# A hybrid decoder trunk on one core: the branch for overfull experts moves from behind the experts to in front of them

## Chip, cores and metric

The kernel runs on one core of a Trainium2 chip. The metric is the device time of one execution in microseconds, as the median over several runs.

## What is computed

Two decoder layers over 512 tokens of width 1024 in float32. Layer 0 mixes tokens by a gated delta rule, layer 1 by sparse attention. Behind each mixer stand a scaled residual, a layer norm, and a mixture of experts: of 16 experts in 4 groups every token takes the two best of its best group, each with hidden width 256.

```python
def hier_moe(x, w_grp, b_grp, w_rt, b_rt, w_gate, w_up, w_down):
    ...
    gate = jnp.sum(jax.nn.one_hot(expert_id, MOE_EXPERTS, dtype=jnp.float32) * top_w[..., None], axis=1)
    def step(acc, e_in):
        wg, wu, wd, ge = e_in
        hdn = jax.nn.silu(xt @ wg) * (xt @ wu)
        return acc + ge[:, None] * (hdn @ wd).astype(jnp.float32), None
```

The reference computes every expert for every token with a gate that is mostly zero; the kernel computes an expert only for the tokens that chose it.

## The kernel before, in words

A matrix product in float32 is made of three passes: each operand is split into a high part (a cast on ScalarE, `split`, L243) and the rest (a subtraction on VectorE or POOL, L252), and TensorE multiplies high by high, low by high and high by low (`mm3`, L276 to L278). In the trace wh and wl are the parts of gate and up weights, dh and dl of down weights, hgh and hgl of the gathered tokens.

`choose` (L907) picks two experts per token on VectorE and gives every token a slot in its expert; an expert has HOT = 128 slots, and tokens past the 128th have a slot number of 128 or more (`spos`). `moe` (L1113) then makes the lists of tokens (`idx`, L1119) and the largest number of tokens of any expert (`cm`, and `cmi` as an integer, L1124 to L1128). After that come the 16 experts in a software pipeline. `expert` (L1034) is a generator; each `go` advances it by a step: gather of its 128 tokens from d_h by an indirect DMA on POOL (L1039), transposes (L1049) with hgh and hgl behind them (L1053, L1054), gate and up (L1058), the activation (L1064 to L1066), its transposes (L1071), down (L1087), the product with the gate weight (L1095), and a scatter that adds the rows to the accumulator `d_acc` in HBM (L1101). The last experts (three in layer 0, two in layer 1, `late`) keep their rows in SBUF (L1089, L1090); `moe_finish` (L1332) brings them to the tokens by one-hot matmuls (L1350 in layer 0, L1387 in layer 1), adds them to h (L1355, L1394) and norms. h has by then been loaded from d_h and the accumulator has been added to it by a DMA from POOL (`addacc`, L1206 to L1213).

Weights come in loads of 1 MB on SP's queue (`load`, L1172; two issues for gate and up in L198, one for down in L208) into 13 raw buffers: three in the ring "raw", seven in "raw2", three in "raw3". Which one a load takes is worked out in `raw_slot` (L225); of the first five loads (gate and up of experts 0 and 1, down of expert 0) all take "raw2". From expert 3 on a load also waits until the load two before has landed (`paced`). The parts wh and wl have four buffers each, dh and dl two.

Inside each engine a scheduler orders the instructions at compile time by its own estimate, apart from those that `keep_in_program_order` holds in the order written. The parts of the first expert's weights (L1198, L1199) are held like this, and behind the fourth of them eight one-hots of 128x128 on VectorE (`slot_onehots`, L1143), which give the gate weight of each slot (`slot_weights`, L991).

Tokens past slot 128 are treated in a branch (L1280 to L1313) that stands behind all experts. Each engine loads `cmi` into a register and compares it with HOT. The body computes, for the slots 128 to 511 in three rounds of 128, the token lists, then loops over the experts, loads the weights again, and writes the rows to a buffer `d_yo` in HBM; after the loop every token gathers its own rows from there and adds them to h. The tiles of the body come out of the same rings as those around it. An engine that skips the body runs a few semaphore instructions instead (also put down to L1281), by which its semaphores get the counts that the body would have given them; those of SP wait for the DMA queues, those of POOL for its own DMAs. No instruction of another part stands between those of the body.

What ends a layer: in layer 0 `prefetch` (L1842) loads the first weights of the next stage from ScalarE's queue (L1844) ahead of the branch in the text, and `moe_finish` stands behind it; in layer 1 `moe_finish` writes the output.

## Time and profile before

| | us |
|---|---|
| median of 3 runs | 1187.27 |
| the runs | 1184.38, 1187.27, 1199.31 |
| profiled execution | 1185.92 |
| its span, first to last instruction | 1184.1 |
| experts of layer 0 (first gather to last late output) | 418.3 to 597.0 |
| experts of layer 1 | 972.4 to 1151.5 |

The profile is of one execution. PE is TensorE's matmuls, PEld its weight loads, DVE VectorE, ACT ScalarE, POOL GpSimd, SP SyncE; a name with q (PEq, PEldq, DVEq) is that engine's queue, which runs loads of registers, compares and semaphores, and these are not counted as busy. A row of the timeline gives start, duration, engine, line, operation, output and inputs, the number of instructions that are merged into it, and in brackets how long the engine had stood idle and what ended that. A row of the waits gives who waited for what, the total in us, how often, and the longest. A row of a line (its own view) gives the number of instructions, the shortest, median and longest duration in ns, and the first and last start in us.

### The profile page before, as it was taken

The numbers are of one execution on the slowest core, as the hardware profiler recorded it, in microseconds if no ns is written. First come the engines' busy times: TensorE is split into PE (matmuls) and PEld (weight loads), VectorE is DVE, ScalarE is ACT, GpSimd is POOL, SyncE is SP. The second block draws the span as 40 slices with busy tenths as digits, with TensorE's granted clock in tenths as the row PEclk, the third lists the DMA queues.
The fourth block names the chain that finished last, engine by engine and source line by source line (L and its number), as shares of the span: only waits on it lengthen the run. The fifth ranks groups of instructions, "written<-read, shape, count | busy, mean of one in ns | idle before, by whom it ended". The sixth has DMA issues, their size and how long they took to land. (4 is left out here: it accounts for less than half of the span.)

```text
span 1184.1 us, 16377 instructions
## 1 busy us (share of the span) xinstructions
PE 1068.6 (90%) x5565; PEld 843.7 (71%) x5565; DVE 837.4 (71%) x1511; ACT 609.9 (52%) x1085; POOL 540.2 (46%) x456
## 2 busy tenths in 40 slices
PE   6898999999999769999978999999999949989974
PEld 4677888788787557777766867667776837777763
DVE  3797777556563779999984224687785477999975
ACT  3532433232441259888722243477884036888862
POOL 0623873301002239888623213045545035888854
PEclk9998999999999979999999999999999978999997
DMA  6532434431126898999872582211115867899963
GB/s 211 174 102 78 112 96 119 163 97 39 36 72 191 290 324 280 297 311 304 249 214 84 149 249 99 71 37 28 37 49 157 306 211 266 286 288 307 332 147 97
DMA packets 110079, 206.01 MB, mean 174 GB/s; under 512 B 34473, under 2 KB 65321, under 8 KB 105892
## 3 DMA queue, kind: packets, MB, share of 16 engines
q1 hardware_dynamic: 96180, 178.18, 45.4%
q0 software_dynamic: 9584, 19.36, 7.2%
q10 hardware_dynamic: 4224, 7.34, 2.2%
q8 instruction: 47, 0.77, 0.3%
q14 instruction: 44, 0.36, 0.1%
HBM read 190.66 MB, written 35.21 MB: 191 GB/s over the span
## 5 line engine op out<-in xcount | busy, mean ns | idle before, releaser
L243 ACT CAST wh<-raw 128x1024 fp32r<-128x1024 f32 (+3 forms) x218 | 205.5, 949 | 189.3 <-PE mm L277 106.2
L252 DVE TENSOR_TENSOR wl<-raw,wh 128x1024 fp32r<-128x1024 f32 (+2 forms) x173 | 228.2, 1335 | 74.5 <-ACT wh L243 55.0
L276 PE MATMUL mm<-xh,wh 128*128 128x512 f32 (+2 forms) x400 | 165.9, 415 | 4.2 <-ACT wh L243 4.2
L278 PE MATMUL mm<-xh,wl 128*128 128x512 f32 (+2 forms) x400 | 162.9, 408 | 0.9 <-DVE wl L252 0.9
L277 PE MATMUL mm<-xl,wh 128*128 128x512 f32 (+2 forms) x400 | 163.4, 409 | 0.0
L252 POOL TENSOR_TENSOR wl<-raw,wh 128x1024 fp32r<-128x1024 f32 (+1 forms) x37 | 101.3, 2739 | 50.3 <-ACT wh L243 38.8
L1721 POOL TENSOR_SCALAR s<-s,st,gate 128x256 f32<-128x256 f32 (+2 forms) x96 | 64.5, 684 | 90.2 <-PE mm L1698 45.3
L276 PEld LDWEIGHTS mm<-xh,wh 128*128 128x128 f32 (+2 forms) x400 | 75.9, 190 | 24.8 <-ACT wh L243 4.8
L278 PEld LDWEIGHTS mm<-xh,wl 128*128 128x128 f32 (+2 forms) x400 | 75.7, 189 | 18.9 <-DVE wl L252 1.4
L277 PEld LDWEIGHTS mm<-xl,wh 128*128 128x128 f32 (+2 forms) x400 | 75.8, 189 | 16.3
L252 POOL TENSOR_TENSOR dl<-raw,dh 128x1024 fp32r<-128x1024 f32 x29 | 71.1, 2452 | 31.3 <-ACT dh L243 30.6
L1709 DVE CUSTOM_DVE_ANT_0 s<-mm,bias 128x128 f32<-128x128 f32 (+3 forms) x128 | 60.2, 481 | 24.3 <-PE tp L1726 20.8
L252 DVE TENSOR_TENSOR dl<-raw,dh 128x1024 fp32r<-128x1024 f32 x35 | 75.7, 2171 | 1.8 <-ACT dh L243 1.8
L1713 ACT ACTIVATE s<-s,st 128x128 f32<-128x128 f32 (+3 forms) x128 | 71.4, 559 | 8.8 <-DVE st L1709 8.4
L1101 POOL DMA_INDIRECT d_acc<-ye,idx x27 | 55.6, 2061 | 41.2 <-ACT ehh L1074 16.4
L243 ACT CAST dh<-raw 128x1024 fp32r<-128x1024 f32 x64 | 66.7, 1046 | 4.9 <-PE mm L278 1.3
L1039 POOL DMA_INDIRECT hg<-d_h,idx x32 | 56.8, 1776 | 17.1 <-ACT wh L243 7.5
L777 POOL TENSOR_TENSOR ln_m<-ln_m,mh 128x1 f32<-128x1 f32 x16 | 15.9, 991 | 102.9 <-DVE ln_m L776 102.9
L278 PE MATMUL mm<-wh,hgl 128*128 128x512 f32 x128 | 52.9, 413 | 11.0 <-DVE hgl L1054 11.0
L1726 PE MATMUL tp<-cst,s 128*128 128x128 f32 x320 | 55.2, 274 | 0.5 <-ACT cpt L1678 0.2
L1697 PE MATMUL mm<-kh,q 128*128 128x256 f32 (+2 forms) x128 | 53.9, 422 | 0.3 <-DVE st L1709 0.2
L276 PE MATMUL mm<-wh,hgh 128*128 128x512 f32 x128 | 52.6, 411 | 0.0
(505 smaller groups left out, 2682.1 us busy)
## 6 DMA issues: line engine op xcount, KB each, us to landing
raw<-in_moe_w_down_dram SPq DMA_DIRECT2D x32, 1024.0 KB, 6.9
raw<-in_moe_w_gate_dram SPq DMA_DIRECT2D x64, 512.0 KB, 6.5
raw<-in_moe_w_up_dram SPq DMA_DIRECT2D x64, 512.0 KB, 7.0
raw<-in_gdn_w_in_dram SPq DMA_DIRECT2D x16, 1024.0 KB, 6.9
d_h<-raw SPq DMA_DIRECT2D x10, 512.0 KB
d_sk<-d_rr ACTq DMA_DIRECT2D x4, 1280.0 KB, 25.8
bc<-d_gc SPq DMA_DIRECT2D x16, 256.0 KB
d_acc<-u SPq DMA_DIRECT2D x8, 512.0 KB, 5.6
```

The costliest lines, as they stand in the source:

```text
L243: p(nc.scalar.copy(h, src))
L252: p(e.tensor_tensor(l, src, h, op=OP.subtract))
L276: nc.tensor.matmul(ps, a[0], b[0], start=start, stop=False)
L277: nc.tensor.matmul(ps, a[0], b[1], start=False, stop=False)
L278: nc.tensor.matmul(ps, a[1], b[0], start=False, stop=stop)
L1039: nc.gpsimd.indirect_dma_start(out=hg, out_offset=None, in_=d_h, bounds_check=T - 1, oob_is_err=False, in_offset=bass.IndirectOffsetOnAxis ...
L1101: i = nc.gpsimd.indirect_dma_start(out=dst, out_offset=bass.IndirectOffsetOnAxis(ap=to, axis=0), in_=ye, in_offset=None, compute_op=OP.add ...
L1697: nc.tensor.matmul(a.ps[:, :W], q[:, c], kh[:, :W], start=True, stop=False)
L1709: nc.vector.tensor_tensor_reduce(out=a.p, in0=a.ps[:, :a.W], in1=bias[a.head][:, (3 - a.i) * P:], scale=-1.0, scalar=3e38, op0=OP.add, op1 ...
L1713: nc.scalar.activation(a.p, a.p, AF.Exp, bias=a.st[:, 0, a.i:a.i + 1], scale=-1.0, accum_out=a.st[:, 1, a.i:a.i + 1])
L1721: en.tensor_scalar(a.p, a.p, a.st[:, 2, a.i:a.i + 1], N["gate"][:, a.i, k:k + 1], op0=OP.mult, op1=OP.mult)
L1726: nc.tensor.transpose(a.ps[:, j * P:(j + 1) * P], a.p[:, j * P:(j + 1) * P], self.ident)
```

## The change

The branch moves from behind the experts to between the gather of the first expert and that of the second; five loads of weights are issued ahead of it (`load` skips those that have been made). Its body is now the function `overflow`. In place of the buffer `d_yo` and the gathers out of it, the body computes the gate weight of every slot past 128 (24 more one-hots and small matmuls in three rounds, kept in `d_gs`), and its experts scale their rows and add them to the accumulator by the same scatter as the others. Its weights take the three buffers of the ring "raw", and its gathers the second of the two token buffers. The scatter in the body isn't held in program order (`pin=None`).

```diff
--- before.py
+++ after.py
@@ -1024,6 +1024,38 @@
         half = lambda i: lambda w=None: self.raw((g[:, 4 * i:4 * i + 4, :], u[:, 4 * i:4 * i + 4, :]), (KC, EH), w)
         return half(0), half(1), lambda w=None: self.raw(src[2].rearrange("(p j) c -> p j c", j=2), (2, D), w)
 
+    def overflow(self, ep, R, d_h, hg):
+
+        nc, tc, layer = self.nc, self.tc, R["layer"]
+        NJ = CAP // HOT
+        d_io = self.t(self.dr, [P, NJ, E], f"d_io{layer}", I32)
+        d_gs = self.t(self.dr, [P, NJ, E], f"d_gs{layer}")
+        for j in range(1, NJ):
+            pi, pw = self.bank("tp", 3), self.bank("tp", 3)
+            for tt in range(NT):
+                self.slot_ids(ep, R, tt, j, pi[:, :E])
+            for tt in range(NT):
+                for i in range(2):
+                    o, pj = self.t(ep, [P, P], "oh32", bufs=2 * NT), self.t(ep, [P, 1], "opj", bufs=2)
+                    nc.vector.tensor_scalar(pj, R["spos"][:, i, tt:tt + 1], float(-j * HOT), None, op0=OP.add)
+                    nc.vector.tensor_scalar(o, self.c["iota"], pj, None, op0=OP.is_equal)
+                    nc.tensor.matmul(pw[:, :E], o, R["A"][:, i, tt, :], start=tt + i == 0, stop=tt + i == NT)
+            io, gw = self.t(ep, [P, E], "oi", I32, 2), self.t(ep, [P, E], "og", bufs=2)
+            nc.vector.tensor_scalar(io, pi[:, :E], float(NOWHERE), None, op0=OP.add)
+            nc.vector.tensor_copy(gw, pw[:, :E])
+            nc.sync.dma_start(d_io[:, j, :], io)
+            nc.sync.dma_start(d_gs[:, j, :], gw)
+        with tc.For_i(0, E, 1) as e:
+            r = [a(self.slot(1)) for a in self.expert_weights(layer, e)]
+            gu = [self.split_gu(r[i // 2], i, ["dve"] * 4) for i in range(4)]
+            dn = self.split_dn(r[2], ["dve"] * 2)
+            for j in range(1, NJ):
+                io, gw = self.t(ep, [P, 1], "oi1", I32, 2), self.t(ep, [P, 1], "og1", bufs=2)
+                nc.sync.dma_start(io, d_io[:, j, bass.ds(e, 1)])
+                nc.sync.dma_start(gw, d_gs[:, j, bass.ds(e, 1)])
+                for _ in self.expert(ep, hg, gu, lambda: dn, io, d_h, R["acc"], io, gs=gw, pin=None):
+                    pass
+
     def split_gu(self, raw, i, lo=LO):
         r = raw.rearrange("p (a b) c -> p a b c", a=2)
         return self.spl2(r[:, :, i % 2 * 2:i % 2 * 2 + 2, :], lo[i])
@@ -1100,7 +1132,7 @@
                 yield
                 i = nc.gpsimd.indirect_dma_start(out=dst, out_offset=bass.IndirectOffsetOnAxis(ap=to, axis=0), in_=ye,
                                              in_offset=None, compute_op=OP.add, bounds_check=T - 1, oob_is_err=False)
-                if CFG["spin"]:
+                if CFG["spin"] and pin is not None:
                     self.tc.keep_in_program_order(i)
 
     def onehot(self, R, tt, e, pin=False):
@@ -1126,8 +1158,6 @@
         nc.vector.tensor_reduce(cm, ps[:, :E], axis=AX.X, op=OP.max)
         cmi = self.t(mp, [P, 1], "cmi", I32)
         nc.vector.tensor_copy(cmi, cm)
-        d_yo = self.t(self.dr, [E * (CAP - HOT), D], f"d_yo{layer}")
-        d_io = self.t(self.dr, [P, CAP // HOT, E], f"d_io{layer}", I32)
         with self.pool("ep", "right") as ep:
             X, R["late"] = {}, []
             self.t(ep, [P, D], "ye", bufs=CFG["ye"])
@@ -1171,9 +1201,10 @@
 
             def load(e, n):
                 if e < E:
-                    if n == 0:
+                    if e not in raws:
                         raws[e] = list(self.expert_weights(layer, e))
-                    raws[e][n] = raws[e][n]()
+                    if callable(raws[e][n]):
+                        raws[e][n] = raws[e][n]()
 
             def spread():
                 for i in range(4):
@@ -1183,9 +1214,12 @@
                     nc.scalar.copy(gb[:, c], ps)
 
             raws = {}
-            load(0, 0)
-            load(0, 1)
+            for e, n in ((0, 0), (0, 1), (1, 0), (1, 1), (0, 2)):
+                load(e, n)
             tokens(0)
+            n = nc.values_load(cmi[0:1, 0:1], min_val=0, max_val=T)
+            with tc.If(n > HOT):
+                self.overflow(ep, R, d_h, hgs[1])
             for e in range(1, CFG["hg"]):
                 tokens(e)
             if CFG["o32e"] == 1:
@@ -1277,40 +1311,6 @@
             for i in range(2):
                 R["pre"](i)
             self.pace = 0
-            n = nc.values_load(cmi[0:1, 0:1], min_val=0, max_val=T)
-            with tc.If(n > HOT):
-                for j in range(1, CAP // HOT):
-                    pi = self.bank("tp", 3)
-                    for tt in range(NT):
-                        self.slot_ids(ep, R, tt, j, pi[:, :E])
-                    io = self.t(ep, [P, E], "oi", I32, 2)
-                    nc.vector.tensor_scalar(io, pi[:, :E], float(NOWHERE), None, op0=OP.add)
-                    nc.sync.dma_start(d_io[:, j, :], io)
-                with tc.For_i(0, E, 1) as e:
-                    a, b, d = self.expert_weights(layer, e)
-                    gu = []
-                    for r in (a, b):
-                        r = r(self.slot(2))
-                        gu += [self.split_gu(r, len(gu) + i, ["dve"] * 4) for i in range(2)]
-                    dn = self.split_dn(d(self.slot(2)), ["dve"] * 2)
-                    for j in range(1, CAP // HOT):
-                        io = self.t(ep, [P, 1], "oi1", I32, 2)
-                        nc.sync.dma_start(io, d_io[:, j, bass.ds(e, 1)])
-                        for _ in self.expert(ep, hgs[j % CFG["hg"]], gu, lambda: dn, io, d_h, d_yo[bass.ds(e * (CAP - HOT) + (j - 1) * HOT, HOT), :]):
-                            pass
-                f8 = lambda a: a.rearrange("p a b -> p (a b)")
-                go, so = self.t(ep, [P, 2, NT], "ogo"), self.t(ep, [P, 2, NT], "oso")
-                soi = self.t(ep, [P, 2, NT], "osoi", I32)
-                nc.vector.tensor_scalar(f8(so), f8(R["spos"]), -float(HOT), 0.0, op0=OP.add, op1=OP.max)
-                nc.vector.scalar_tensor_tensor(f8(soi), f8(R["sbase"]), (CAP - HOT) / HOT, f8(so), op0=OP.mult,
-                                               op1=OP.add)
-                nc.vector.scalar_tensor_tensor(f8(go), f8(R["spos"]), float(HOT), f8(R["gate"]), op0=OP.is_ge, op1=OP.mult)
-                for tt in range(NT):
-                    for i in range(2):
-                        y = hgs[i]
-                        nc.gpsimd.indirect_dma_start(out=y, out_offset=None, in_=d_yo,
-                                                     in_offset=bass.IndirectOffsetOnAxis(ap=soi[:, i, tt:tt + 1], axis=0))
-                        nc.vector.scalar_tensor_tensor(h[tt], y, go[:, i, tt:tt + 1], h[tt], op0=OP.mult, op1=OP.add)
             self.ring = 1
 
     @contextmanager
```

## Rows read from the trace of the kernel before

**Rows 1.** The page, part 1: busy time, share of the span, instructions of each engine.

```profile
PE 1068.6 (90%) x5565; PEld 843.7 (71%) x5565; DVE 837.4 (71%) x1511; ACT 609.9 (52%) x1085; POOL 540.2 (46%) x456
```

**Rows 2.** Waits of TensorE, 950 to 1158 us: total, times, longest.

```profile
PE mm L1387 <- PEq L1281: 6.2, 1, 6.2
...
PE tp L1049 <- DMA hg<-d_h,idx: 6.1, 1, 6.1
```

**Rows 3.** Waits of TensorE, 404 to 600 us.

```profile
PE tp L1049 <- DMA hg<-d_h,idx: 8.8, 1, 8.8
...
PE o L1350 <- DVEq L1281: 2.1, 1, 2.1
```

**Rows 4.** Line L1281, layer 1: duration ns min/median/max, first and last start.

```profile
L1281 PEldq COMPARE_BRANCH  x1: 6159/6159/6159, 1149.6 to 1149.6; - x1
...
L1281 DVEq COMPARE_BRANCH  x1: 68/68/68, 1151.8 to 1151.8; - x1
...
L1281 PEldq EVENT_SEMAPHORE  x1: 51/51/51, 1155.8 to 1155.8; - x1
```

**Rows 5.** Line L1281, layer 0.

```profile
L1281 SPq EVENT_SEMAPHORE  x8: 17/17/17, 570.9 to 600.5; - x8
...
L1281 PEldq COMPARE_BRANCH  x1: 367/367/367, 594.5 to 594.5; - x1
...
L1281 ACTq COMPARE_BRANCH  x1: 45/45/45, 596.6 to 596.6; - x1
```

**Rows 6.** Timeline, end of layer 1: start, duration, engine, line.

```profile
1149.83 1.63 DVE L1090 SCALAR_TENSOR_TENSOR raw<-mm,rgs,raw 128x512 fp32r<-128x512 f32 x2 [2.14 <-ACT raw L1089]
...
1156.17 5.97 PE L1387 MATMUL mm<-raw,raw 128*128 128x512 f32 x16 [6.21 <-PEq L1281]
...
1158.25 0.69 DVE L1394 TENSOR_TENSOR raw<-mm,raw 128x512 f32<-128x512 f32 x1 [6.78 <-PE mm L1387]
```

**Rows 7.** Line L1394, the closing norm's first add in layer 1.

```profile
L1394 DVEq EVENT_SEMAPHORE  x1: 49/49/49, 1155.5 to 1155.5; - x1
```

**Rows 8.** Timeline of VectorE, end of layer 0.

```profile
596.27 0.75 DVE L1090 SCALAR_TENSOR_TENSOR raw<-o,rgs,raw 128x512 fp32r<-128x512 f32 x1 [0.19 <-ACT raw L1089]
...
599.30 0.69 DVE L1355 TENSOR_TENSOR raw<-o,raw 128x512 f32<-128x512 f32 x1 [2.28 <-DMA raw<-d_acc]
...
605.59 1.23 DVE L252 TENSOR_TENSOR wl<-raw,wh 128x1024 fp32r<-128x1024 f32 x1 [0.65 <-ACT wh L243]
```

**Rows 9.** Timeline, start of the experts of layer 0.

```profile
415.31 3.87 ACT L243 CAST wh<-raw 128x1024 fp32r<-128x1024 f32 x4
...
417.39 0.14 DVE L1128 CAST cmi<-cm 128x1 int32<-128x1 f32 x1
...
421.03 4.45 DVE L1143 TENSOR_SCALAR oh<-cst,rspos 128x128 f32<-128x128 f32 x8
...
427.77 0.69 DVE L1054 TENSOR_TENSOR hgl<-tp,hgh 128x512 fp32r<-128x512 f32 x1 [2.28 <-ACT hgh L1053]
```

**Rows 10.** Line L1280, the load of the count on TensorE, layer 1.

```profile
L1280 PEldq TENSOR_LOAD <-cmi x1: 1717/1717/1717, 1147.8 to 1147.8; - x1
```

**Rows 11.** Timeline, start of the experts of layer 1.

```profile
969.44 3.87 ACT L243 CAST wh<-raw 128x1024 fp32r<-128x1024 f32 x4
...
971.63 0.15 DVE L1128 CAST cmi<-cm 128x1 int32<-128x1 f32 x1
...
971.77 3.49 DVE L252 TENSOR_TENSOR wl<-raw,wh 128x1024 fp32r<-128x1024 f32 x3
...
975.18 4.46 DVE L1143 TENSOR_SCALAR oh<-cst,rspos 128x128 f32<-128x128 f32 x8
...
979.56 1.28 DVE L1054 TENSOR_TENSOR hgl<-tp,hgh 128x512 fp32r<-128x512 f32 x2
```

**Rows 12.** DMA issues, 900 to 971.6 us: count, KB each, us to landing.

```profile
raw<-in_moe_w_up_dram SPq DMA_DIRECT2D x10, 512.0 KB, 5.8
...
raw<-in_moe_w_down_dram SPq DMA_DIRECT2D x4, 1024.0 KB
```

**Rows 13.** Busy us by engine, TensorE's clock, DMA share, GB/s, 470 to 560 us.

```profile
470.00:560.00 90.00, 84.95 (x404) 68.46 (x404) 86.80 (x77) 77.80 (x105) 77.80 (x35) 1.00 0.91 308
```

## Prediction

> **What bounds the kernel now.** I read first how busy the engines are over the whole span: TensorE runs matmuls for 1068.6 of 1184.1 us [rows 1]. The kernel is bound by TensorE, so a change is worth what it does to TensorE's gaps. Second I read the list of waits of TensorE in the two stretches with the experts. In layer 1 two gaps stand out, 6.2 us before L1387, released by TensorE's own queue at L1281 (the branch), and 6.1 us before the first expert's transposes, released by the gather of its tokens [rows 2]. In layer 0 the same two are 2.1 us and 8.8 us [rows 3]. The change touches just these four places: it takes the branch away behind the experts and puts it in front of them. Third I read the branch line itself, per engine and layer, and fourth the order of time around the four places. No line of the branch's body (L1282 to L1313) is in the trace: no expert has over 128 tokens with these inputs, and that doesn't change. So what counts is what a branch costs that is not taken.

> What it costs in time: every engine loads the count into a register (L1280), compares (L1281), and then raises its semaphores by as much as the body would have done. The compare took 0.05 to 0.07 us on VectorE and ScalarE; on TensorE it took 6.159 us in layer 1 [rows 4] and 0.367 us in layer 0 [rows 5]. An instruction behind the branch that shares a buffer with the body waits for the raised count of the engine that uses it there: TensorE's L1350 waits 2.1 us for VectorE's branch [rows 3]. This is the mechanism on which the sum rests.

> **Part 1, the end of layer 1: the branch goes.** VectorE's last late output ends at 1149.83 + 1.63 = 1151.46, TensorE then stands until 1156.17, and VectorE's first add of the closing norm starts at 1158.25 [rows 6]. Without the branch TensorE starts L1387 when those outputs are there. What is late next is the transfer that adds the accumulator into h (L1213): VectorE's queue passes its wait for the first half at 1155.5 [rows 7]. So the add moves from 1158.25 to 1155.5, a gain of 2.75; I take 2.8. The bounds are 0 (if the transfer turns out later) and 6.8 (all from 1151.46 on).

> **Part 2, the end of layer 0.** VectorE ends its last late output at 596.27 + 0.75 = 597.02 and starts the first add at 599.30, after 2.28 idle; later it stands 0.65 for a cast of the next stage's weights [rows 8], whose transfers on ScalarE's queue are behind the branch and wait there for SP, which passes its eight semaphores only at 600.5 [rows 5]. Both go: 2.9 us, bounds 0 and 2.9. The two ends together give 5.7 us.

> **Part 3, the start of layer 0: the branch comes.** The count (cmi, L1128) is there at 417.39 + 0.14 = 417.53. Before, ScalarE cast the first expert's weights from 415.31 on, and VectorE's first hgl, which lets TensorE go on, started at 427.77 after 2.28 us with nothing to do [rows 9]; the gather covered that. Now the casts write the four wh buffers that the body's matmuls also read, so they wait for TensorE's branch: load of the count 1.72 [rows 10], compare 0.37 [rows 5], some 0.2 around them, so 419.8. Then four casts, 3.87 [rows 9], to 423.7; the last wl behind them, 3.49/3 = 1.2 [rows 11], to 424.9; eight one-hots on VectorE, 4.45 [rows 9], to 429.35. The hgl comes 1.6 us later than now. Bounds: 0 (all stays hidden) and 7.3 (the compare takes 6.16 here as well).

> **Part 4, the start of layer 1.** The count is there at 971.63 + 0.15 = 971.78. Here VectorE had no slack: hgl starts at 979.56, as the one-hots end [rows 11]. I take for this layer the long compare that it has now: 971.85 + 1.72 + 6.16 + 0.1 = 979.8; casts 3.87 to 983.7; wl 1.2 to 984.9; one-hots 4.46 to 989.4. That is 9.8 us later. Bounds: 0 and 9.8; with the short compare it is 4.0. Behind ScalarE's waiting casts stand the copies hgh, behind VectorE's wl the one-hots and hgl, and TensorE waits for hgl. On POOL the branch waits for the landing of the first gather before it lets the second through, but that one isn't wanted before TensorE has done the first expert, some 9 us on: nothing.

> [...]

> **Part 5, the loads.** SP's loads of expert weights used to run ahead without a stop: in layer 1 nine and a half gate and up MB and four of down are issued before the choice ends [rows 12]. Now five are sure to be; the rest come behind the branch if the body's three weight buffers stand in their way: up to 8.5 MB later in layer 1, some 6 in layer 0. Cost nothing, since TensorE works: the first missing one is wanted with the second expert, over 14 us after SP is through, and the transfers then catch up, as they run at 308 GB/s and 0.91 busy in the steady stretch [rows 13], that is up to 308/0.91 = 338. An expert needs 3.15 MB, 9.3 us of that, in a period of some 10.4. Without that cover: rival D. The smaller edits (gate sums in the branch, the accumulating scatter there, no pin) run only inside a branch that isn't taken: nothing.

> **Sum.** 1.6 + 9.8 - 2.8 - 2.9 = +5.7 us. The profiled execution took 1185.92 us (span 1184.1 and 1.8 around it): 1191.6. It stands 1.35 us under the median of the runs shown, 1187.27, so the change would hardly show.

> **Rivals.**
> A. Both layers get the long compare. For: the body grows by 24 small matmuls with their weight loads, so the jump is longer, and one of two is long already. Against: layer 0 has the short one now. Part 3 becomes 7.3: 1185.9 + 7.3 + 9.8 - 5.7 = 1197.3. It decides if TensorE's compare in layer 0 is over about 2 us. [...]
> B. Both get the short compare; not slower. Place: the same compare at the start of layer 1. For: VectorE and ScalarE have it in the rows, and TensorE in layer 0. Against: TensorE's place and its jump in layer 1 stay alike. Then part 4 is 4.0: 1185.9 + 1.6 + 4.0 - 5.7 = 1185.8, no change. From a compare under about 0.5 us this one decides.
> C. The casts aren't held, because the order puts them, or the hgl ahead of the one-hots, where the branch doesn't bind. For: they are ready at 415.3 and 969.4. Against: the buffers. Then only the ends count: 1180.2.
> D. The lost lead of the loads isn't made up. For: the transfer engines are at 0.91 already. Against: no wait of TensorE for a weight stands in [rows 2, 3]. 14.5 MB at 338 GB/s are 43 us, less a cover of 13 per layer: 17 on top, 1208.
> That the change does nothing would need the branch to be free in both places; the gaps in [rows 2] speak against it.

> **How the numbers follow.** Forecast 0.45, A 0.18, B 0.2, C 0.1, D 0.05, anything else 0.02. The likeliest gives 1191.6; its own range is 1187 to 1195. For 8 in 10 I go to C below and past A above: 1179 to 1201. Two per cent is 23.7 us, about what a measurement of this kernel can tell from no change, as its three runs lie 15 us apart. None of A, B, C or the forecast leaves it; D comes near the upper end: faster 0.02, within 0.92, slower 0.06.

> **What would show it.** The compare of TensorE in front of layer 1's first expert near 6.2 us and in layer 0 near 0.4; the first cast of wh right behind it in both; the first hgl about 1.6 and 9.8 us later after the count than now. At the ends no line of the branch, the first add of layer 1 starting as the accumulator's transfer lands, some 4 us after the last late output. Wrong would be a cast of the first expert before TensorE is through the branch, a TensorE wait for weights of the second to fifth expert, or an add at the end that starts much later than the last output plus 4 us.

## The result and the profile after

| | us |
|---|---|
| median before, over 4 runs | 1190.39 |
| median of the changed kernel, over 4 runs | 1202.9 (1199.83 to 1209.27) |
| ratio | 1.0115, interval 1.0074 to 1.0156 |
| the same kernel in two later series of 12 runs each | 1.0085 (1.005 to 1.0119), 1.0071 (1.0035 to 1.0107) |
| profiled execution, its span | 1209.27, 1207.5 |

By the medians the change costs 12.5 us in this series and 10.1 and 8.7 in the later ones, one and a half to two times the forecast of +5.7, and the median here lies above the range. The profiled execution is the slowest of the four, so its span stands 23 us above that of before, and not all of that belongs to the change. The places have to be read one by one.

The page of the changed kernel, part 1, answers to [rows 1]: TensorE is busy for 13 us more with the same number of matmuls.

```profile
PE 1081.8 (90%) x5565; PEld 852.2 (71%) x5565; DVE 841.9 (70%) x1511; ACT 608.9 (50%) x1085; POOL 541.1 (45%) x456
```

The waits of TensorE, 404 to 612 us, answer to [rows 3]:

```profile
PE o L278 <- DVE hgl L1086: 11.6, 7, 6.1
...
PE tp L1081 <- PEq L1221: 4.9, 1, 4.9
```

and those of 985 to 1005 us to [rows 2]:

```profile
PE mm L278 <- DVE hgl L1086: 6.1, 1, 6.1
```

In both layers a new wait of 6.1 us stands at the start, for the first hgl; the 6.2 us for the branch at the end of layer 1 are gone. The branch line, by engine, shows the load of the count first (L1220, its own view) and then the compare and the raised semaphores (L1221). It answers to [rows 4, 5, 10]:

```profile
L1220 PEldq TENSOR_LOAD <-cmi x2: 312/400/487, 418.1 to 984.1; - x2
```

```profile
L1221 DVEq COMPARE_BRANCH  x2: 68/70/72, 418.7 to 984.5; - x2
L1221 PEldq COMPARE_BRANCH  x2: 3608/3760/3912, 418.7 to 984.5; - x2
...
L1221 DVEq EVENT_SEMAPHORE  x2: 21/21/21, 419.3 to 987.5; - x2
...
L1221 PEldq EVENT_SEMAPHORE  x2: 51/51/51, 422.4 to 988.5; - x2
...
  ACT wh L243: 13.4, 2
```

TensorE's compare is long in both layers, 3.61 and 3.91 us, and its semaphore follows at 422.4 and 988.5. The last line (who waited for this line) names the casts of the first expert. VectorE's compare row is short in both, but in layer 1 its semaphore comes 3 us behind it. The timeline of the start of layer 0 answers to [rows 9]:

```profile
417.94 0.14 DVE L1160 CAST cmi<-cm 128x1 int32<-128x1 f32 x1
...
422.54 3.89 ACT L243 CAST wh<-raw 128x1024 fp32r<-128x1024 f32 x4 [6.58 <-PEq L1221]
...
425.56 2.64 POOL L252 TENSOR_TENSOR wl<-raw,wh 128x1024 fp32r<-128x1024 f32 x1 [1.21 <-ACT wh L243]
...
426.46 2.82 DVE L252 TENSOR_TENSOR wl<-raw,wh 128x1024 fp32r<-128x1024 f32 x1 [0.48 <-ACT wh L243]
...
429.21 4.41 DVE L1173 TENSOR_SCALAR oh<-cst,rspos 128x128 f32<-128x128 f32 x8
...
433.54 1.27 DVE L1086 TENSOR_TENSOR hgl<-tp,hgh 128x512 fp32r<-128x512 f32 x2
...
434.27 0.80 PE L278 MATMUL o<-wh,hgl 128*128 128x512 f32 x1 [6.08 <-DVE hgl L1086]
```

This is the predicted chain: compare, four casts, the last wl, eight one-hots, hgl. From the end of the count (418.08) to the first hgl it takes 15.46 us, before 10.24. The wl at 426.46 takes 2.82 us instead of 1.2; POOL's wl runs beside it, and it ends 1.1 us after that one. In this layer the gather no longer covers anything: TensorE's transposes start 4.6 us after the count (422.67), as TensorE leaves its own branch (the wait of 4.9 us above), and before they started 8.5 us after it, behind the gather. Layer 1 has the same chain, and answers to [rows 11]; count to hgl 15.57 us, before 7.78:

```profile
983.89 0.15 DVE L1160 CAST cmi<-cm 128x1 int32<-128x1 f32 x1
...
988.61 3.88 ACT L243 CAST wh<-raw 128x1024 fp32r<-128x1024 f32 x4 [6.79 <-PEq L1221]
...
992.52 2.83 DVE L252 TENSOR_TENSOR wl<-raw,wh 128x1024 fp32r<-128x1024 f32 x1 [0.48 <-ACT wh L243]
...
999.61 1.27 DVE L1086 TENSOR_TENSOR hgl<-tp,hgh 128x512 fp32r<-128x512 f32 x2
```

The clock is the second part of it. Busy time in stretches of 4 us, the granted clock third from the right, before and after the change, each beginning behind TensorE's return (427.79 before, 434.27 after):

```profile
428.00:432.00 4.00, 4.00 (x14) 3.14 (x15) 1.52 (x3) 1.70 (x3) 1.01 (x1) 0.73 0.83 304
432.00:436.00 4.00, 4.00 (x26) 3.52 (x25) 2.27 (x3) 3.32 (x4) 1.48 (x1) 1.00 0.96 367
```

```profile
436.00:440.00 4.00, 4.00 (x12) 3.14 (x12) 1.23 (x1) 2.09 (x2) 0.00 (x0) 0.59 0.90 359
440.00:444.00 4.00, 4.00 (x30) 3.63 (x28) 2.17 (x2) 3.07 (x5) 2.25 (x1) 1.00 0.98 317
444.00:448.00 4.00, 3.24 (x13) 2.35 (x13) 3.22 (x6) 0.56 (x2) 1.92 (x2) 0.77 0.90 338
```

Before, the clock is full from 432 on. After the longer stop it comes back later (0.59 from 436 to 440, full from 440 on) and falls a second time (0.77), so the first two experts are slower too. From the first hgl to that of the third expert the mean granted clock was 0.94 (layer 0) and 0.91 (layer 1) before, over 19.7 and 20.2 us. In the three profiles of the changed kernel it was 0.78 to 0.80 in five of the six starts, over 22.7 to 23.2 us, and 0.90 in the sixth, over 20.4 us. Part of TensorE's added busy time is this.

The ends. Layer 1 answers to [rows 6], layer 0 to [rows 8]:

```profile
1175.58 4.12 PE L1387 MATMUL mm<-raw,raw 128*128 128x512 f32 x16
1175.62 1.64 DVE L1122 SCALAR_TENSOR_TENSOR raw<-mm,rgs,raw 128x512 fp32r<-128x512 f32 x2 [2.14 <-ACT raw L1121]
...
1180.42 0.69 DVE L1394 TENSOR_TENSOR raw<-mm,raw 128x512 f32<-128x512 f32 x1 [3.16 <-DMA raw<-d_acc]
```

```profile
611.19 0.75 DVE L1122 SCALAR_TENSOR_TENSOR raw<-kq,rgs,raw 128x512 fp32r<-128x512 f32 x1 [0.18 <-ACT raw L1121]
...
611.85 0.68 DVE L1355 TENSOR_TENSOR raw<-o,raw 128x512 f32<-128x512 f32 x1
```

In layer 1 TensorE goes on at once, and the first add waits for the accumulator's transfer alone: 3.16 us after the last late output instead of 6.79. In layer 0 the add follows the last output without a stop.

The places, each worked out from two rows of the timeline (its two ends), for the profile before and the three of the changed kernel:

| stretch | before | changed |
|---|---|---|
| layer 0, count to first hgl of the third expert | 29.9 | 38.2, 38.3, 38.8 |
| layer 1, the same | 28.0 | 38.5, 36.0, 37.8 |
| last late output of layer 0 to the count of layer 1 | 374.8 | 372.1, 371.7, 372.3 |
| last late output of layer 1 to the end | 32.6 | 30.2, 32.1, 30.6 |
| third expert to last hgl, both layers | 273.0 | 281.8, 272.6, 282.3 |
| start of the program to the count of layer 0 | 417.5 | 418.1, 414.3, 414.6 |

The starts cost 18.0 us on the mean (8.5 and 9.5), the ends give 4.4 (2.7 and 1.7): +13.6. The stretch inside the experts moves by 10 us from one execution of the same kernel to the next, and the stretch ahead of the first count lay between 412.2 and 422.8 us in the sixteen profiles of this document, so neither can be put down to the change from one profile of before. The starts and ends hold against a second base: with the kernel that has the branch put back (below) they come to +18.6 and -4.8.

### The profile page after: what moved, and what is told of

Its sections match the earlier page's. It is cut to its first block, busy times and chain, and to the rows that moved or that the text cites. A ratio compares the mean times of both kernels' runs of the same rounds, so it can differ in the third digit from the quotient of the medians.

```text
span 1207.5 us, 16391 instructions
## 1 busy us (share of the span) xinstructions
PE 1081.8 (90%) x5565; PEld 852.2 (71%) x5565; DVE 841.9 (70%) x1511; ACT 608.9 (50%) x1085; POOL 541.1 (45%) x456
## 5 line engine op out<-in xcount | busy, mean ns | idle before, releaser
L252 DVE TENSOR_TENSOR wl<-raw,wh 128x1024 fp32r<-128x1024 f32 (+2 forms) x173 | 235.5, 1375 | 92.4 <-ACT wh L243 74.9
L277 PEld LDWEIGHTS mm<-xl,wh 128*128 128x128 f32 (+2 forms) x400 | 75.9, 190 | 16.4
```

Source lines behind the costliest of these rows:

```text
L252: p(e.tensor_tensor(l, src, h, op=OP.subtract))
L277: nc.tensor.matmul(ps, a[0], b[1], start=False, stop=False)
```

## Experiments

The count is the end of the cast of cmi; the first hgl is VectorE's first one behind it.

### The changed kernel twice again, without the branch, with the branch put back, with hgl ahead

`a_again` and `a_again2` are the changed kernel itself.

> The changed kernel itself, unaltered, for more times and a second profile; it leaves nothing out. The profiled execution of it shows TensorE's matmuls drift against before by some 6.7 us at the first expert of layer 0, 10.5 us at that of layer 1, -2.7 and -2.4 us at the two ends, and by 4 to 6 us inside the experts of layer 0 and 3 us inside those of layer 1. Theory S (the starts): the two starts come out alike in every execution, compare on TensorE 3.6 to 3.9 us, first hgl some 15.5 us after the count; the drift inside the experts is different from execution to execution, so the ratio to before is 1.010 to 1.013, and the second profile shows another number of gaps of 1.9 us before hgl than the nine of the first. Theory L (the lost lead of the loads, rival D of the prediction): nine gaps or close to it again, at about the same experts, and the drift inside the experts again 7 us or more in all.

> The changed kernel itself again, on the same chip as the two others. Both theories: ratio 1.007 to 1.013, first hgl 15.4 to 15.6 us after the count in both layers. The stretch of the experts (first hgl of the third expert to the last hgl), which was 141.3 and 140.5 us in the first profile and 137.5 and 135.1 in the second: theory S, anywhere in 134 to 142, like before and the kernels without a branch; theory L, above 138 in both layers.

Measured: 1.0085 and 1.0071; first hgl 15.4 to 15.6 us (first series) and 15.6 and 15.1 us (second) after the count. The starts come out alike each time, though the first ratio lies a little under the 1.010 expected and the 15.1 under its 15.4. Of the gaps of 1.9 us inside the experts the profile above has seven (the nine of the expectation include two at the starts), these two have one and six. The stretch of the experts is short in one and long in the other, as the table above shows, so theory L's "above 138 in both layers" holds in one of them alone.

Without the branch:

```diff
             tokens(0)
-            n = nc.values_load(cmi[0:1, 0:1], min_val=0, max_val=T)
-            with tc.If(n > HOT):
-                self.overflow(ep, R, d_h, hgs[1])
```

> The changed kernel without load of the count, compare and body: tokens past slot 128 would be left out (no expert has any with these inputs). The five early loads stay. Theory S: both starts go back to what they were before the change (first hgl some 10 and 8 us after the count), both ends stay without the branch, so the time is that of before less 5 us: ratio 0.994 to 0.998. Theory L says nothing against that, since no load is held here, but then the gaps of 1.9 us inside the experts should be two or fewer, as in the profile of before; if five or more stand here too, the lead isn't their cause.

> The kernel without the branch again, for more times on the same chip as the held loads and a second profile (tokens past slot 128 left out, of which there are none). Both theories: ratio to before 0.988 to 0.996, first hgl 9.3 and 7.9 us after the count, no compare.

Measured: 0.9898 (0.9846 to 0.995) and 0.9927 (0.9895 to 0.9959), so 8.7 to 12.1 us under before, more than the 5 expected. By the four places above, its two profiles stand 7.3 and 10.0 us under before: 3.4 and 4.6 at the end of layer 0, 2.9 and 3.0 at that of layer 1, and 1.0 and 2.4 at the starts. The starts go back to those of before (first hgl 9.3 and 7.9 us after the count, in the second profile 7.9 and 7.9), and from layer 0's last output to layer 1's count it takes 371.4 and 370.2 us. Against the changed kernel this is 17 to 22 us; the two starts are 19 and 20 of it. Three and four gaps of 1.9 us or more stand inside the experts here, with no load held back.

The branch with its new body back behind the experts:

> The branch with its new body put back behind the experts, the five early loads kept; its weights go into the ring raw2 there, as in the old body. Place against body: if the place costs (both theories) the ratio is 0.998 to 1.002 and TensorE's compare in layer 1 shows whether the longer body makes it longer than 6.16 us. If the new body or the reordered loads cost by themselves, 1.005 or more.

Measured: 0.9995 (0.9965 to 1.0025). So the place costs, not the body and not the order of the loads. TensorE's compare in layers 0 and 1 (the branch line in two stretches):

```profile
L1312 PEldq COMPARE_BRANCH  x1: 5017/5017/5017, 601.1 to 601.1; - x1
```

```profile
L1312 PEldq COMPARE_BRANCH  x1: 328/328/328, 1158.4 to 1158.4; - x1
```

Long and short have changed layers against [rows 4, 5] (0.367 and 6.159). Which layer has the long jump was thus no property of the layer: it changed with the program.

The one-hots behind hgl on VectorE (the two hgl are held in program order as well):

```diff
-                if i == CFG["o32e"] - 2:
-                    slot_onehots()
             ...
             go(0)
+            slot_onehots()
```

> The changed kernel with the eight one-hots of the first expert behind its two hgl on VectorE instead of ahead of them; nothing is left out. Theory S: the chain compare, casts, wl, one-hots, hgl is what TensorE waits for, so taking 4.4 us of one-hots out of it moves the first hgl 4.4 us up in both layers; with some clock won back 8 to 11 us less than the changed kernel: ratio to before 1.002 to 1.005. Theory L: the loads, not the chain, set when the experts go on, and little of it arrives at the end: 1.009 or more.

Measured: 1.0013 (0.9976 to 1.0051), 7 to 9 us less than the changed kernel in the same series, as theory S has it. The start of layer 0:

```profile
415.07 0.14 DVE L1162 CAST cmi<-cm 128x1 int32<-128x1 f32 x1
...
420.01 3.88 ACT L243 CAST wh<-raw 128x1024 fp32r<-128x1024 f32 x4 [6.93 <-PEq L1223]
...
426.68 1.28 DVE L1086 TENSOR_TENSOR hgl<-tp,hgh 128x512 fp32r<-128x512 f32 x2
```

The casts are as late as ever (4.8 us after the count), the hgl is 4.0 earlier (4.6 in layer 1). The chain is what TensorE waits for.

### Is it the jump? Another layout, and hints

```diff
-            with tc.If(n > HOT):
+            with tc.If(n > HOT, preferred_fallthrough_block=False):
```

> The changed kernel with one edit: the way past the body is laid out as the next instructions behind the compare, and the body behind it, so that an engine that skips the body first raises its semaphores and then jumps. Nothing is left out. Theory F (the 3.6 to 3.9 us of TensorE's compare are the jump to instructions that aren't at hand, and the casts wait for the semaphore behind it): the compare takes under 0.4 us in both layers, TensorE raises its semaphore some 3.4 us earlier, the first cast starts 1.0 to 1.4 us after the count instead of 4.5, the first hgl 12.0 to 12.5 us after it instead of 15.5, and the time falls by 7 to 9 us: ratio to before 1.001 to 1.004. The jump itself may stay long behind the semaphore; there the gather covers it. Rival W (the compare is long because TensorE waits for something else there, or the casts wait for another engine): compare or casts stay where they are and the ratio is 1.008 to 1.012.

> The kernel with the way past the body next behind the compare, again, for a second profile and more times. By its starts (first hgl 9.3 and 13.1 us after the count) and its ends it should stand at 1.001 to 1.004 (theory S); the first time it was measured at 1.0082 with an interval from 1.0046. If it comes out at 1.006 or more again, some 5 us of the change are not explained by the starts; if the stretch of the experts is again some 8 us longer than before in its second profile, they lie there.

The branch line and the start of layer 0 (first series):

```profile
L1221 PEldq COMPARE_BRANCH  x4: 81/1879/3767, 415.7 to 971.2; - x4
...
L1221 PEldq EVENT_SEMAPHORE  x2: 51/51/51, 415.8 to 971.1; - x2
```

```profile
414.91 0.14 DVE L1160 CAST cmi<-cm 128x1 int32<-128x1 f32 x1
...
416.10 3.88 ACT L243 CAST wh<-raw 128x1024 fp32r<-128x1024 f32 x4 [3.17 <-PEq L1221]
...
422.75 1.65 DVE L1173 TENSOR_SCALAR oh<-cst,rspos 128x128 f32<-128x128 f32 x8
...
424.31 1.27 DVE L1086 TENSOR_TENSOR hgl<-tp,hgh 128x512 fp32r<-128x512 f32 x2
```

There are now two jumps on each engine: a short one, 0.08 to 0.10 us on TensorE, then the semaphore, then the long one of up to 3.77. The time has moved with the jump and not with the compare. The casts start 1.05 and 1.18 us after the count, and rival W falls. Layer 0's first hgl is at 9.26, as without a branch. In layer 1 it is at 13.14. There VectorE's own jump shows, between its semaphore at 971.0 and its first wl in the timeline:

```profile
974.39 5.66 DVE L252 TENSOR_TENSOR wl<-raw,wh 128x1024 fp32r<-128x1024 f32 x3 [3.83 <-ACT wh L243]
...
983.63 1.28 DVE L1086 TENSOR_TENSOR hgl<-tp,hgh 128x512 fp32r<-128x512 f32 x2
```

Compare, semaphores and casts did what theory F says; the first hgl came at neither start at the 12.0 to 12.5 us expected, but earlier in layer 0 and later in layer 1. The time came out less well: 1.0082 (1.0046 to 1.0117) and 1.0054 (1.0027 to 1.0082), above the 1.001 to 1.004 expected. Part of that is the expectation's: it left out what follows the first hgl, where the first two experts of layer 1 took another 3 us. By the first four lines of the table this kernel stands 4 us over before in both its profiles. The rest of the 6 to 10 us measured lies within the intervals, or inside the experts (281.2 and 283.8 us in its two profiles).

A hint that the jump will be taken, on TensorE's queue alone and then on all five:

```diff
-            with tc.If(n > HOT):
+            with tc.If(n > HOT, label=f"of{layer}"):
...
+            tc.mark_branch_hint_location(f"of{layer}", "LikelyTaken", [nc.tensor.engine])
             raws = {}
```

> The changed kernel with a hint on TensorE's queue that the branch will be taken past the body. The scheduler puts it far ahead: in layer 0 as the first instruction of the program, in layer 1 right behind the branch of layer 0. Nothing is left out. Theory F: if the hint brings the target in and it is still there when the branch comes, the compare takes under 0.4 us in either layer and the ratio is 1.001 to 1.004 as with the other layout; if what it brings in is replaced by the thousand instructions between, the compare stays at 3.6 to 3.9 us and the ratio at 1.008 to 1.012. Rival W: no change either way, so only a short compare tells.

> The changed kernel with the hint that the branch is taken past the body on the queues of all five engines instead of TensorE's alone; nothing is left out. Theory F (jump to instructions not at hand): on TensorE alone the hint had made the compare short in both layers (0.39 and 0.36 us), and what held the casts then was VectorE, whose semaphore came 3.7 and 4.8 us after the count, its jump. With the hint on VectorE too, both semaphores come 0.9 to 1.3 us after the count in both layers, the first cast starts 1.0 to 1.6 us after it, and the first hgl comes 9.2 to 11 us after it; by the starts and ends the ratio is 0.996 to 1.001, and 1.002 to 1.006 if theory L's loads cost on top. Rival V (VectorE is late for another reason than its jump): its semaphore stays 3.5 us or more behind the count in layer 1 and the ratio above 1.008.

On TensorE alone:

```profile
L1222 PEldq COMPARE_BRANCH  x2: 365/376/388, 417.8 to 979.0; - x2
...
L1222 DVEq EVENT_SEMAPHORE  x2: 21/21/21, 420.8 to 983.3; - x2
```

The hint is an instruction of its own on TensorE's queue. It stands at 0.8 us and at 418.4, some 417 and 560 us ahead of its branch:

```profile
L1904 PEldq BRANCH_PREFETCH_HINT  x2: 36/43/50, 0.8 to 418.4; - x2
```

On all five:

```profile
L1222 PEldq EVENT_SEMAPHORE  x2: 51/51/51, 418.3 to 980.2; - x2
...
L1222 DVEq EVENT_SEMAPHORE  x2: 21/21/21, 418.5 to 980.3; - x2
```

TensorE's compare is short with the hint in both layers. With TensorE alone it does not help (1.0123, 1.0086 to 1.016, against the 1.001 to 1.004 expected of a short compare): the casts now wait for VectorE, whose semaphore comes 3.65 and 4.76 us after the count. With the hint on VectorE too it comes 1.27 and 0.99 us after the count, the casts start at 1.44 and 1.17, and the ratio is 1.0012 (0.9985 to 1.004). Rival V falls. The first hgl is at 9.4 us in layer 1, but at 12.4 in layer 0, outside the 9.2 to 11 expected: there the eight one-hots take 4.41 us, since a dl of POOL runs beside them, against 1.65 in layer 1.

With the new body TensorE's long compare takes 3.3 to 5.0 us, with a hint 0.36 to 0.39 us. The traces list the loading of instructions as DMA queues of their own, and a transfer on one of them goes with the long compare. In TensorE's compare of layer 0 in the changed kernel (418.74 to 422.35) there stands, with packets, MB and share:

```profile
q8 instruction: 1, 0.02, 2.2%
```

In the thirteen profiles with a branch TensorE has 18 long compares, of 3.3 to 6.2 us, and in each of them just one transfer on q8 falls; in the 14 short ones, of 0.39 us and less, none does. By chance it would be about one in seven (an estimate: 48 such transfers in 1207.5 us, against 3.6 us). Which engine q8 serves the trace does not say; that the long compare waits for this transfer is the author's reading of these counts and of the hints.

### The shared buffers

```diff
-            gu = [self.split_gu(r[i // 2], i, ["dve"] * 4) for i in range(4)]
+            gu = []
+            for i, y in enumerate([self.slot(3), self.slot(3), self.slot(3), self.slot(2)]):
+                v = r[i // 2].rearrange("p (a b) c -> p a b c", a=2)[:, :, i % 2 * 2:i % 2 * 2 + 2, :]
+                h, l = (y[:, k * 1024:(k + 1) * 1024].bitcast(F32R).rearrange("p (a c b) -> p a c b", a=2, c=2) for k in range(2))
+                self.split((h, l), v, "act", "dve")
+                gu.append((h, l))
```

> The changed kernel, but the body writes the parts of its gate and up weights into four raw buffers (three of raw3, one of raw2) instead of the four wh and wl buffers that the first expert uses; compare, place and loads are unchanged, nothing is left out. Theory H (hold: the start is late because the first casts write buffers that the skipped body reads, so they wait for TensorE's raised count): the compare still takes 3.6 us or more, but the first cast starts some 2.2 us before the count as without a branch, the first hgl comes 9.3 to 10 us (layer 0) and 7.8 to 9 us (layer 1) after the count, and the ratio to before is 0.988 to 0.996, as without the branch. Rival P (TensorE's own stop, or VectorE's, sets the start, whatever the buffers): the first hgl 12 us or more after the count, ratio 1.000 or more.

Measured: 1.0146 (1.0093 to 1.02), the contrary of what I expected; by its numbers (first hgl 12.6 and 13.1 us after the count) rival P came. The start of layer 0:

```profile
414.74 0.14 DVE L1165 CAST cmi<-cm 128x1 int32<-128x1 f32 x1
...
415.51 4.10 ACT L243 CAST wh<-raw 128x1024 fp32r<-128x1024 f32 x4 [2.76 <-DVE rlid L1001]
...
420.79 6.90 DVE L1178 TENSOR_SCALAR oh<-cst,rspos 128x128 f32<-128x128 f32 x8
...
421.80 2.39 POOL L252 TENSOR_TENSOR wl<-raw,wh 128x1024 fp32r<-128x1024 f32 x1
...
427.48 1.27 DVE L1091 TENSOR_TENSOR hgl<-tp,hgh 128x512 fp32r<-128x512 f32 x2
```

and VectorE in layer 1 (count at 972.89):

```profile
976.82 3.50 DVE L252 TENSOR_TENSOR wl<-raw,wh 128x1024 fp32r<-128x1024 f32 x3 [3.85 <-DVEq L1226]
```

The first half of theory H holds: with a long compare on TensorE (3.33 us) the casts start 0.63 us after the count, so it was the shared buffers that held them. They are not 2.2 us ahead of the count, as expected, since ScalarE runs the branch itself: its compare stands at 415.5, the first cast at 415.51. But the first hgl gains only 2.9 us in layer 0 (12.6), because POOL's wl and dl now fall beside the one-hots and stretch them to 6.90. In layer 1 rival P is right about VectorE: its first wl waits for its own branch, 3.9 us after the count, and the one-hots take 5.86. And the edit costs the loads: of SP's issues of expert weights, counted from 72 us ahead of layer 0's count on, 11 stand ahead of the count instead of 18, as the raw buffers are in use by the body, and the 27th comes 32.5 us after the count instead of 15.4. This run moved two things at once, so its time settles neither.

### The lost lead of the loads

The kernel without the branch, its first load past the five held until the count is there:

```diff
...
+            self.tc.add_manual_dep(ins.ins, self.hold_on.ins.name,
+                                   mybir.DependencyInfo(mybir.DependencyClass.Sync, mybir.DependencyReason.DATA),
+                                   reason="held")
...
```

> The changed kernel without the branch (load of the count, compare and body left out), and with the first expert load behind the five early ones made to wait for the count, so that SP's loads lose the lead that they lose in the changed kernel, and nothing else. Theory L (rival D of the prediction: the lost lead isn't made up): 6 to 10 us more than the same kernel without the wait, with the loss inside the experts, ratio to before 0.996 to 1.002. Theory S: the loads catch up beside the experts, as the prediction costed them; within 3 us of the kernel without the wait, ratio 0.987 to 0.996.

Measured: 0.9959 (0.9928 to 0.999) beside 0.9927 for the same kernel without the wait, in one series: medians 1183.44 and 1180.92. That is 2.5 us, 3.8 by the ratios, with a place: the gather of the first expert in layer 1, which now runs beside the held loads. TensorE's wait there in the list of waits, held and then not held:

```profile
PE tp L1091 <- DMA hg<-d_h,idx: 9.5, 1, 9.5
```

```profile
PE tp L1081 <- DMA hg<-d_h,idx: 6.1, 1, 6.1
```

Inside the experts nothing is lost (274.3 us held, 274.6 and 279.6 not held). In the changed kernel's layer 1 TensorE waits only 5.6 us for the gather, so even this part isn't paid there. But the run takes back only a part of the lead: counted as above, SP's 27th issue comes in layer 1 6.9 us after the count without the wait, 14.9 with it and 22.0 in the changed kernel; in layer 0 it is 11.7 and 12.3 without, 13.2 with and 15.4. So it doesn't settle theory L by itself. Two other things speak against it. Inside the experts of the changed kernel's profile no wait of TensorE, ScalarE or VectorE ends with a weight transfer: ScalarE's casts wait for TensorE, TensorE for hgl. And `a_best` below issues its loads nearly as late as the changed kernel (16.4 and 20.1 us) and is no slower than before. Theory L's 6 to 10 us are not there.

### Versions that give the starts back

Both edits of the layout and of hgl together (`a_fallhgl`), and the hints on all queues with hgl first (`a_best`):

> The changed kernel with both edits that moved its starts: the way past the body next behind the compare, and the one-hots of the first expert behind its two hgl on VectorE. Nothing is left out. With the first edit alone the first hgl came 9.26 us after the count in layer 0 and 13.14 in layer 1, where VectorE's own jump (3.9 us from the count to its first wl) and then 3.7 us of one-hots stood ahead of it. Theory S (only the starts and ends count): the first hgl 9.0 to 9.3 us after the count in layer 0 and 9.3 to 10 in layer 1, and by the stages the time is that of before, plus 0 and 2 at the starts, less 5 at the ends: ratio 0.994 to 1.000. Theory L (the loads that come later behind the branch cost inside the experts, whatever the start): the same starts, but 1.001 to 1.006.

> The changed kernel with the hint on all five queues (both jumps short) and the one-hots behind the first expert's hgl; nothing is left out. If the starts are what the change costs, this takes nearly all of it back: first hgl 8 to 9 us after the count in both layers, the ends stay without a branch, and the time comes under that of before: ratio 0.993 to 0.999. If something else of the change costs as well (theory L, or the stretch between), 1.000 to 1.005.

`a_fallhgl`: 1.0004 (0.9966 to 1.0041), first hgl at 7.7 and 9.2 us after the count. Here and in `a_hints` the end of layer 0 gave nothing back (376.3 and 376.5 us to the count of layer 1): the first cast of the next stage's weights starts 11.6 and 10.7 us after the first of their loads is issued, 6.0 to 6.3 in the three profiles of the changed kernel. The reason is open. `a_best`: 0.997 (0.9935 to 1.0006), median 1186.51 beside 1191.45 of before; the first hgl is at 8.1 us in layer 0, and in layer 1, in the timeline, at 8.8:

```profile
978.25 0.15 DVE L1162 CAST cmi<-cm 128x1 int32<-128x1 f32 x1
...
987.16 0.69 DVE L1086 TENSOR_TENSOR hgl<-tp,hgh 128x512 fp32r<-128x512 f32 x1 [0.88 <-ACT hgh L1085]
```

This version is faster than the changed kernel in the same series (1.0071, 1.0035 to 1.0107) and no slower than the one before, with the branch in its new place. The starts are what the change cost.

## Why the prediction failed

**Direction and chain** were right: the kernel stays within 2 per cent, the casts wait for TensorE's branch, TensorE waits for hgl, and both ends give something back. As a difference, the forecast of +5.7 us stands against +12.5 in the first series, +10.1 and +8.7 in the others, and against +13.6 by the places. Of the 7.9 us between +5.7 and +13.6, a missing term is 5.0, the first hgl 1.5 and the ends 1.3.

**The step that failed first is part 3**, the compare of 0.37 us in layer 0 [rows 5]. It was 3.61. That it was short before had been taken for a property of the layer, and the branch put back shows that it changes with the program (5.02 us in layer 0, 0.33 in layer 1). Together with the last wl (+1.6) and the load of the count (-1.2) this made part 3 +5.2 at the first hgl instead of +1.6.

**A term was put at nothing**, and in the time it is the largest miss: what follows the first hgl. Up to the third expert the starts cost another 3.2 (layer 0) and 1.8 us (layer 1, means of three profiles), as the clock comes back later and falls again: in the profile above 2.7 and 2.1 us of it are longer busy time of TensorE (21.67 instead of 18.97 us, 21.48 instead of 19.40), at a mean clock of 0.80 and 0.79 instead of 0.94 and 0.91. The prediction priced the stop of TensorE as time lost and gave no reason for leaving the clock out. With the branch put back this stretch is as long as before (40.0 us in both layers together, 39.9 before, 44.9 in the changed kernel), so the 5.0 does not hang on one profile.

**The other sizes in the chain** made up for part 3 by luck. The load of the count took 0.49 and 0.31 us, not the 1.72 of [rows 10]; layer 1's compare 3.91, not 6.16 [rows 4]; the last wl 2.8, not 1.2, beside POOL's. So part 4 is +7.8 instead of +9.8, and both together +12.9 on the mean, where +11.4 was forecast.

**Rival A** named the long compare in layer 0 ("over about 2 us") and gave 1197.3, +11.4. Its condition came. That its sum is near is luck as well: it has 17.1 us for the two starts from a compare of 6.16, which nowhere stood there, and the starts cost 12.9 and then 5.0 behind the first hgl. That a longer body makes the jump longer is not shown: the long compare took 6.16 us before and 5.02 with the new body put back. It got 0.18, though only one of two rows of TensorE was short.

**The ends**: part 2 gave 2.7 of 2.9, part 1 on the mean 1.7 of 2.8, its profiles lying between 0.6 and 2.4. The first add came 3.16 us after the last late output, under the 4 us named as the sign.

**Part 5 and rival D**: the loads cost nothing worth naming, as forecast: the wait for weights that would have shown it wrong did not come, and the loads held in part cost 2.5 us, none of it inside the experts. Rivals B and C did not come: no compare was short, and no cast started ahead of the branch.

**The range** ended at 1201.0, 3.7 above rival A, and was built on a profiled execution of 1185.92. The median of before in the first series was 1190.39. The ratio times 1185.92 would have been inside; the absolute time was not. A range in us has to hold the spread of the base as well.

**Open** is how much the stretch inside the experts differs between the kernels. It ran from 268.6 to 283.8 us over sixteen profiles, with one profile for most kernels. Much of the spread goes with TensorE's clock, and not with the kernel: the thirteen layers with a mean granted clock of 1.00 took 133.6 to 137.6 us each, the seven with 0.96 to 0.98 took 139.1 to 146.2, and both kinds are found in the kernels with and without a branch at the start (the branch put back has 279.3 in all and the time of before). What makes the clock fall there is not shown.

## What to carry to other kernels

A branch whose body never ran still held up the work that waits for its semaphores: here the first casts started 4.5 and 4.6 us after the count, before 2.2 and 2.3 us ahead of it. Before moving one, list the buffers that its body shares with the work behind it, and look for a long jump on each engine: here TensorE's compare took 3.61 and 3.91 us and VectorE's semaphore came 2.9 us after its compare in layer 1; with a hint on all five queues TensorE's took 0.39 us and less, and VectorE's semaphore came 1.27 and 0.99 us after the count. A place where every engine has work in hand should be better, by the author's guess; no run here tried one. Where TensorE's stop grows at a start, read the granted clock behind it as well: here the stretch behind the first hgl cost another 5.0 us on 12.9, with a mean clock of 0.78 to 0.80 in five of six starts.
